# A hybrid pooling and RWKV-7 encoder: two recurrences side by side, their products by turns, with six value groups spread beside them

## The chip, the cores and the metric

The kernel runs on one core of one Trainium2 chip. TensorE (PE) multiplies, VectorE (DVE) and ScalarE (ACT) do the element-wise work and empty PSUM, GpSimd (POOL) does a few small copies, and SyncE (SP) issues most transfers. Each engine executes its own queue in order; semaphores tie the queues together. The metric is the device time of one execution in microseconds (us), as a median of runs.

## The reference

One sequence of 256 tokens of width 2048 goes through two layers. The first mixes tokens by causal pooling, the second by an RWKV-7 recurrence; each is followed by a gated feed-forward block. The part that matters here is the recurrence of the second layer:

```python
def step(state, inp):
    r_t, w_t, k_t, v_t, a_t, b_t = inp
    sa = jnp.einsum('bhvk,bhk->bhv', state, a_t)
    state = (state * w_t[:, :, None, :] + sa[..., None] * b_t[:, :, None, :]
             + v_t[..., None] * k_t[:, :, None, :])
    return state, jnp.einsum('bhvk,bhk->bhv', state, r_t)
...
_, y = lax.scan(step, state0, seq_in)
...
y = (y + bonus.reshape(B, S, D)).astype(h.dtype)
return (y * g) @ w_o
```

There are 32 heads of 64 channels. Ahead of it stand the products r, k, v of the shifted tokens with 2048 x 2048 weights, two small low-rank products for decay and a (`w_la`, `a_la`) and one for the gate (`g_la`); behind it a norm per head, the gate, and the output product with `w_o`.

## The kernel before

The recurrence is done in chunks of 64 tokens. Four heads make a group; there are eight groups, and each has a chain of four chunks in order of time. All activations of a stage stay on the chip, weights are streamed in pieces of 512 KB (`raw`), and each piece is split into a high part (ACT, line 152) and a low remainder (DVE, line 153), so that a product of two float32 numbers becomes three fast ones.

The second layer runs in this order: `keys` and `receptances` (products for k and r, 16 of each), `values` (eight groups of four pieces), `prepare` (decayed k and r of a group, written to memory as dKB and dM), `invert` (solves all 64-by-64 triangular systems of half the heads by 31 pairs of DVE instructions), `ready` (loads a group's operands back, makes its Gram matrices G and its inverses Z), `chains` (the recurrence), `head_norm` with `gating`, and `out_proj`.

One chunk of a chain has three phases, each ended by a `yield`. Phase 0 (lines 905 to 912): products of G with the values, of AR with the state S, and a copy on ACT to `rhs`. Phase 1 (lines 915 to 917): products with Z and a copy back to the value rows. Phase 2 (lines 920 to 937): products with G and with KBT, four updates of S on DVE, a scaled copy `Se`, and the copy of the result to `y`. A product in float32 is issued as two matmul instructions. Chunk c reads one half of the 128 rows where c is even and the other where it is odd (`kh[c % 2]`).

What runs beside what is written by hand. `weave(main, *others)` walks a main generator step by step; each of the others has a count of units, a first step and a last step, and is advanced evenly between them. This fixes the program order. When the program is built, each engine's queue is put in order from it: a scheduler goes by program order as priority (`high_priority(HP)` moves instructions 30 places ahead) and by its own estimate of when operands and buffers are ready. Tiles with a tag share a number of buffers and wait for a free one.

Before, a chain starts every `STAG` = 8 steps and takes 12, so that two chains are live in half of the 68 steps, out of phase. `values(0)` to `values(3)`, the low-rank gate product and `invert(0)` precede; six of the 16 units of `values(4)` to `values(7)` run just ahead of the chains and the rest by step 20 (`VL`). `out_proj` for the first two groups starts at step 26. PSUM has three banks for large accumulations (`acc`), three for `g` and two for the chains (`cb`). The tag `mx` has `MX` = 40 buffers of 128 x 512, shared by mixed inputs, r, k, KB, AR, y and others.

```python
more = [(ready(g), 6, STAG * g - STAG, STAG * g - RE) for g in range(1, 8)]
more += [(head_norm(g), 4, STAG * g + 12, STAG * g + 12 + HNL) for g in range(7)]
more += [(vals, 16 - LV, 0, VL), (prep, 28 - LP, 0, PE_), (invert(1), 18, PE_, IE), (reload(), 1, STAG + 12, STAG + 13)]
```

Of the kernel before, what the change touches and what calls it, by code (L numbers as in the profile page):

```python
# [14 lines left out]
ALU = mybir.AluOpType  # L15
# [14 lines left out]
MX = 40  # L30
# [9 lines left out]
OB_ = ((0, 2), (2, 2), (4, 2), (6, 1))  # L40
LASTO = 6
OA, OB = 0, 0
STAG, OG, RE = 8, 2, 0
BANKS = {"acc": 3, "g": 3, "cb": 2}
# [48 lines left out]
def hybrid_encoder(ctx: ExitStack, tc: tile.TileContext, I, out):  # L93
# [6 lines left out]
    base = cp.tile([128, 5120], F32, name="base")  # L100
# [149 lines left out]
    def ffn(layer, each=None):  # L250
        gcol = par[f"g2_{layer}"]
        with ExitStack() as st:
# [4 lines left out]
            rb = base[:, 4864:]  # L257
# [188 lines left out]
    def chained(*gens):  # L446
        for gen in gens:
            yield from gen

    def rwkv():  # L450
        with ExitStack() as st:
# [52 lines left out]
            def values(gi):  # L504
# [3 lines left out]
                for u in range(4):  # L508
# [135 lines left out]
            with tc.tile_pool(name="rp1", bufs=1) as p1:  # L644
# [51 lines left out]
                def loras(srcs, names, m, fns, dsts):  # L696

                    acc = acc_bank()
                    xs = None
# [85 lines left out]
                for k in range(16):  # L785
# [3 lines left out]
                      (loras(I["la"], ("mu_w", "mu_a"), 96, (AF.Tanh, AF.Copy), hid[:2]), 17, LA0, 24),  # L789
# [10 lines left out]
            Z = [c2.tile([128, 8, 64], F32, name=f"Z{q}") for q in range(3)]  # L800
# [19 lines left out]
            def ready(gi):  # L820
# [3 lines left out]
                z = Z[gi % 3]  # L824
                w11 = pt = c2.tile([128, 8, 32], F32, name="w11", tag="w11", bufs=1)
                m12 = c2.tile([128, 8, 32], F32, name="m12", tag="m12", bufs=1)
# [60 lines left out]
            def chains(gi):  # L887

                vt, z, S = vts[gi], Z[gi % 3], Sb[gi % 2]
                ar_, kbt_, g_ = AR[gi], KBT[gi], G[gi]  # L890
                y = ys_raw[gi] = mx(F32, "y")

                sv = (vt, c2.tile([128, 512], F32, name="sv", tag="sv", bufs=3))
                nc.gpsimd.tensor_copy(sv[1][kh[1]], vt[kh[1]])
                odd[gi] = sv[1]
                heads_ = [(jj, slice(hd * 64, hd * 64 + 64), jj * 2 + hd) for jj in range(2) for hd in range(2)]
                Se = None
# [268 lines left out]
```

## Time and profile before

| what | value |
|---|---|
| median of 3 runs | 2182.81 us (2179.54 to 2190.74) |
| the profiled execution | 2181.9 us, span 2180.1 us |
| mean granted TensorE clock | 0.981 |
| busy: PE, PEld, DVE, ACT, POOL | 2116.9, 1843.5, 1553.9, 1147.3, 30.6 us |

PE is the busy time of matmuls, PEld that of loads of their stationary operand, which run beside them. Matmuls overlap, so the duration of one is longer than the distance between two starts. In a row of a group of instructions stand line, engine, operation, operands, shapes and count, then busy us, mean ns, and the idle time of the engine just before with what ended it. In a row of time stand start, duration, engine, line, operation and count. A clock of 1.00 is full speed, 0.50 is half. In a row of waits stand who waited for whom, us in total, times and the longest.

### The profile page before, as it was taken

To read this page: it belongs to the slowest core of one execution; us is meant where nothing else is said; L and a number is where in the kernel's file an instruction comes from. 1 tells how busy PE (TensorE), PEld (TensorE's weight loads), DVE (VectorE), ACT (ScalarE), POOL (GpSimd) and SP (SyncE) were. 2 spreads that over 40 slices of the span, in tenths; PEclk is the share of its full clock that TensorE was granted. 3 is DMA by queue.
4 is the path that set the end of the run, shared out by engine and by line. 5 is a ranking of instruction groups with operands and counts; after the bars stand their busy time and mean duration, and the time that the engine had idled before them with its cause. 6 is when DMAs were issued, how large, how long until landed. Compare 5 with 4: busy or idle time off the path is not lost.

```text
span 2180.1 us, 34748 instructions
## 1 busy us (share of the span) xinstructions
PE 2116.9 (97%) x13318; PEld 1843.5 (85%) x13318; DVE 1553.9 (71%) x2548; ACT 1147.3 (53%) x1884; POOL 30.6 (1%) x72
## 2 busy tenths in 40 slices
PE   7999999999999989999999999999999999999997
PEld 5888888888878879999988778788888888888786
DVE  8666666666787978688866767876666666677886
ACT  5544444444555478766745354554444444445444
POOL 0000000000000000011000000000000000000000
PEclk9999999999999999999998699999999999999999
DMA  6555565665566645466565343446666666655654
GB/s 232 174 187 191 186 191 187 190 187 190 196 198 217 207 155 163 163 210 207 171 218 151 108 121 105 160 121 191 188 189 189 188 189 189 188 191 199 204 202 156
DMA packets 147478, 395.11 MB, mean 181 GB/s; under 512 B 39280, under 2 KB 46832, under 8 KB 147056
## 3 DMA queue, kind: packets, MB, share of 16 engines
q1 hardware_dynamic: 146160, 390.80, 56.2%
q8 instruction: 104, 1.70, 0.3%
q10 hardware_dynamic: 1152, 2.10, 0.3%
q14 instruction: 62, 0.51, 0.1%
HBM read 376.59 MB, written 16.25 MB: 180 GB/s over the span
## 4 chain that ended last, share of the span: by engine, by line
PE 86%; DVE 6%; DMA 4%; ACT 2%; issue 1%; SPq 0%; ACTq 0%; DVEq 0%
PE acc L311 29%; PE acc L347 17%; PE acc L313 15%; PE acc L691 2%; PE acc L689 2%; PE acc L690 2%; DVE wl L153 2%; PE tp L347 2%; PE acc L1022 1%; PE acc L1024 1%; PE acc L1023 1%; DMA raw<-in_w 1%; PE acc L516 1%; PE acc L515 1%; PE cb L907 1%
## 5 line engine op out<-in xcount | busy, mean ns | idle before, releaser
L153 DVE TENSOR_TENSOR wl<-raw,wh 128x1024 fp32r<-128x1024 f32 (+1 forms) x525 | 640.2, 1220 | 432.2 <-ACT wh L152 428.0
L152 ACT CAST wh<-raw 128x1024 fp32r<-128x1024 f32 (+1 forms) x525 | 548.5, 1045 | 648.7 <-PE acc L311 276.9
L311 PE MATMUL acc<-xs,wh 128*128 128x512 f32 x2816 | 710.6, 393 | 3.7 <-DVE xs L266 3.2
L311 PEld LDWEIGHTS acc<-xs,wh 128*128 128x128 f32 x2816 | 504.9, 189 | 94.9 <-DVE xs L266 5.1
L313 PEld LDWEIGHTS acc<-xs,wl 128*128 128x128 f32 x2816 | 384.1, 190 | 27.5
L313 PE MATMUL acc<-xs,wl 128*128 128x256 f32 x2816 | 392.7, 282 | 0.0
L347 PE MATMUL acc<-vh,gT 128*128 128x512 f32 x640 | 184.9, 390 | 0.8 <-ACT vh L152 0.8
L347 PEld LDWEIGHTS acc<-vh,gT 128*128 128x128 f32 x640 | 119.7, 188 | 27.3 <-ACT vh L152 2.6
L691 PE MATMUL acc<-mx,wl 128*128 128x256 f32 x464 | 133.0, 287 | 3.5 <-DVE wl L153 3.5
L689 PE MATMUL acc<-mx,wh 128*128 128x256 f32 x464 | 132.1, 285 | 0.0
L690 PE MATMUL acc<-mx,wh 128*128 128x256 f32 x464 | 131.8, 284 | 0.0
L153 DVE TENSOR_TENSOR vl<-raw,vh 128x1024 fp32r<-128x1024 f32 x80 | 95.5, 1221 | 27.1 <-ACT vh L152 19.7
L347 PE MATMUL acc<-vl,gT 128*128 128x512 f32 x320 | 112.2, 389 | 0.0
L152 ACT CAST vh<-raw 128x1024 fp32r<-128x1024 f32 x80 | 80.9, 1050 | 49.3 <-PE acc L347 22.7
L355 ACT CAST vh<-T 128x1024 fp32r<-128x1024 f32 x56 | 58.9, 1052 | 80.5 <-DVE T L397 43.6
L347 PE MATMUL acc<-wh,gT 128*128 128x512 f32 x320 | 93.8, 390 | 0.7 <-ACT wh L152 0.7
L691 PEld LDWEIGHTS acc<-mx,wl 128*128 128x128 f32 x464 | 88.5, 191 | 5.3 <-DVE wl L153 5.2
L689 PEld LDWEIGHTS acc<-mx,wh 128*128 128x128 f32 x464 | 88.5, 191 | 0.8
L690 PEld LDWEIGHTS acc<-mx,wh 128*128 128x128 f32 x464 | 88.6, 191 | 0.0
L347 PE MATMUL acc<-vh,g 128*128 128x512 f32 x280 | 77.9, 391 | 1.1 <-ACT vh L355 0.6
L516 PE MATMUL acc<-wl,mx 128*128 128x256 f32 x256 | 74.2, 290 | 1.2 <-DVE wl L153 1.1
L515 PE MATMUL acc<-wh,mx 128*128 128x256 f32 x256 | 74.2, 290 | 0.0
(329 smaller groups left out, 3118.5 us busy)
## 6 DMA issues: line engine op xcount, KB each, us to landing
raw<-in_w SPq DMA_DIRECT2D x528, 512.0 KB, 4.4
raw<-in_wk SPq DMA_DIRECT2D x32, 512.0 KB, 3.7
raw<-in_wr SPq DMA_DIRECT2D x32, 512.0 KB, 3.7
raw<-in_wv SPq DMA_DIRECT2D x32, 512.0 KB, 4.0
raw<-in_wo SPq DMA_DIRECT2D x32, 512.0 KB, 3.6
raw<-in_pw SPq DMA_DIRECT2D x8, 512.0 KB, 7.8
dKB<-KB SPq DMA_DIRECT2D x16, 256.0 KB, 3.1
dKB<-AR SPq DMA_DIRECT2D x16, 256.0 KB, 3.7
```

What stands on the lines that cost most here:

```text
L152: nc.scalar.copy(wh[:P, :step], raw[:P, :step])
L153: nc.vector.tensor_sub(wl[:P, :step], raw[:P, :step], wh[:P, :step].bitcast(F32))
L311: nc.tensor.matmul(acc, lhsT=w[:, cs], rhs=xs[q * 4 + kk], start=(q + kk == 0), stop=False, skip_group_check=True)
L313: nc.tensor.matmul(acc[:, :256], lhsT=l[:, cs], rhs=xs[q * 4 + kk][:, :256], start=False, stop=(q + kk == 6), skip_group_check=True)
L347: nc.tensor.matmul(out_, lhsT=lhsT, rhs=rhs, start=start, stop=stop, skip_group_check=True)
L355: nc.scalar.copy(wh, src)
L515: nc.tensor.matmul(av[:, i], lhsT=xh, rhs=w[:, cs], start=(k == 0 and i == 0), stop=False, skip_group_check=True)
L516: nc.tensor.matmul(av[:, i], lhsT=xh, rhs=l[:, cs], start=False, stop=False, skip_group_check=True)
L689: nc.tensor.matmul(acc[:, :256], lhsT=w[:, cs], rhs=xs[k][:, :256], start=(k == 0), stop=False)
L690: nc.tensor.matmul(acc[:, :256], lhsT=w[:, cs], rhs=xs[k][:, 256:], start=False, stop=False)
L691: nc.tensor.matmul(acc[:, :256], lhsT=l[:, cs], rhs=xs[k][:, :256], start=False, stop=(k == 15))
L907: nc.tensor.matmul(cb[:, jj, 0, hc], lhsT=g_[jj][u % 2][k_, c], rhs=rows_of(u)[k_], start=(u == 0), stop=False, skip_group_check=True)
```

## The change

Two lanes take the place of the staggered chains. Lane by lane, `BEGIN` gives the step at which each chain starts; chains 0 and 1 start three steps (one chunk) apart, and each next pair follows as the one before ends, so that two chains are live in all but the first and the last three of 51 steps. Both are always in the same phase and their matmuls are written alternately. `values(0)` and `values(1)` stay ahead; the other six groups are spread until step 39, six units of them just ahead of the chains. The gate's low-rank product moves from beside the first values into `keys`, on a `cb` bank. The output projection goes in blocks of two groups (`range(4 * q, 4 * q + 4)` pairs). Buffers change: `mx` 40 to 36, Z 3 to 4, `w11` and `m12` 1 to 2, `sv` 3 to 4, `Se` 2 to 3, and two places for the norm's gain row `lnx` instead of one.

```diff
-MX = 40
+MX = 36
...
-HP, VL, HNL = 30, 20, 6
-LV, LP, PE_, IE = 6, 14, 8, 16
+HP, HNL = 30, 6
+VF, LV, LP, PE_, IE = 2, 6, 14, 8, 17
+
+BEGIN = (0, 3, 12, 15, 24, 27, 36, 39)
+STEPS = 51
+READY = ((3, 12), (5, 15), (17, 24), (18, 27), (28, 36), (30, 39))
...
-                        vts[gi] = mx(F32, "vt") if gi < 4 else late[0].tile([128, 512], F32, name="vt", tag="vt", bufs=4)
+                        vts[gi] = mx(F32, "vt") if gi < VF else late[0].tile([128, 512], F32, name="vt", tag="vt", bufs=4)
...
                 weave(keys(),
-                      (loras(I["la"], ("mu_w", "mu_a"), 96, (AF.Tanh, AF.Copy), hid[:2]), 17, LA0, 24),
+                      (loras(I["la"], ("mu_w", "mu_a"), 96, (AF.Tanh, AF.Copy), hid[:2], acc_bank), 17, LA0, 22),
+                      (loras(I["ga"], ("mu_g", "mu_g"), 128, (AF.Sigmoid, AF.Sigmoid), hid[2:], cb_bank), 17, 8, 30),
                       (mixes("mu_r", xr), 16, 12, 32))
...
-                weave(chained(values(0), values(1), values(2), values(3)),
-                      (loras(I["ga"], ("mu_g", "mu_g"), 128, (AF.Sigmoid, AF.Sigmoid), hid[2:]), 17, 0, 12),
-                      (invert(0), 18, 0, 14))
+                weave(chained(*(values(g) for g in range(VF))),
+                      (invert(0), 18, 0, 4 * VF))
...
+            def chain_step(phase, lanes):
+                with tc.high_priority(HP):
+                    if phase == 0:
+                        for a in lanes:
+                            a.chunk()
                         for jj, hc, u in heads_:
+                            for a in lanes:
+                                nc.tensor.matmul(a.cb[:, jj, 0, hc], lhsT=a.g[jj][u % 2][a.k, a.c], rhs=a.rows_of(u)[a.k], start=(u == 0), stop=False, skip_group_check=True)
+                        for a in lanes:
+                            if a.c:
+                                for jj in range(2):
+                                    nc.tensor.matmul(a.cb[:, jj, 0], lhsT=a.ar[jj][:, a.c], rhs=a.S[a.c % 2][:, jj], start=False, stop=False, skip_group_check=True)
+                        for a in lanes:
+                            a.rhs = c2.tile([128, 2, 128], F32, name="rhs", tag="rhs", bufs=2)
+                            nc.scalar.copy(a.rhs[a.b], a.cb[a.b, :, 0])
+                    elif phase == 1:
                         for jj, hc, u in heads_:
+                            for a in lanes:
+                                nc.tensor.matmul(a.cb[a.b, jj, 1, hc], lhsT=a.z[a.b, u * 2 + a.i], rhs=a.rhs[a.b, jj, hc], start=True, stop=True, skip_group_check=True)
+                        for a in lanes:
+                            nc.scalar.copy(two(a.row[a.b]), a.cb[a.b, :, 1])
+                    else:
                         for jj, hc, u in heads_:
+                            for a in lanes:
+                                nc.tensor.matmul(a.cb[a.k, jj, 0, hc], lhsT=a.g[jj][u % 2][a.b, a.c, a.k], rhs=a.rows_of(u)[a.b], start=False, stop=True, skip_group_check=True)
+                        for a in lanes:
+                            if a.c < 3:
+                                for jj, hc, u in heads_:
+                                    nc.tensor.matmul(a.cb[hc, jj, 1, :64], lhsT=a.kbt[jj][:, a.c, hc], rhs=a.rows_of(u), start=True, stop=True, skip_group_check=True)
...
             def all_chains():
+                lanes = []
+                for step in range(STEPS):
+                    if step in BEGIN:
+                        lanes.append(Chain(BEGIN.index(step)))
+                    chain_step(step % 3, lanes)
+                    lanes = [a for a in lanes if a.c < 4]
                     yield
...
-                lnx = base[:, 4864:]
+                lnx = base[:, 4672 + gi % 2 * 256:][:, :256]
...
+            second = ready(1)
+            weave(itertools.islice(vals, LV), (itertools.islice(prep, LP), LP, 0, LV), (ready(0), 6, 1, LV), (itertools.islice(second, 3), 3, 3, LV))
+            ended = lambda g: BEGIN[g] + 12
+            more = [(second, 3, 0, 3)] + [(ready(g), 6, *READY[g - 2]) for g in range(2, 8)]
+            more += [(head_norm(g), 4, ended(g), ended(g) + HNL) for g in range(7)]
+            more += [(vals, 4 * (8 - VF) - LV, 0, BEGIN[7]), (prep, 28 - LP, 0, PE_), (invert(1), 18, PE_, IE), (reload(), 1, ended(1), ended(1) + 1)]
+            more += [(out_proj(range(4 * q, 4 * q + 4)), 8, ended(2 * q + 1) + HNL, min(ended(2 * q + 1) + HNL + 12, STEPS)) for q in range(3)]
+            more += [(last_weights(), 4, STEPS - 12, STEPS - 2), (head_norm(7, 0, 1), 4, STEPS - 5, STEPS)]
+            rest.append(out_proj(range(12, 14)))
             weave(all_chains(), *more)
```

The updates of S, `Se` and the copy to `y` are the same per lane as before, lane after lane.

More of the change, by code (lines that the diff above doesn't have):

```diff
@@ L97, in hybrid_encoder @@
     sm = ctx.enter_context(tc.tile_pool(name="sm", bufs=2))
-    base = cp.tile([128, 5120], F32, name="base")
+    base = cp.tile([128, 5184], F32, name="base")
     h = [[base[:, (i * 4 + n) * 512:(i * 4 + n + 1) * 512] for n in range(4)] for i in range(2)]
@@ L256, in ffn @@
             ps = st.enter_context(tc.tile_pool(name="fps", bufs=1, space=PSUM))
-            rb = base[:, 4864:]
+            rb = base[:, 4864:5120]
             xs = []
@@ L823, in ready @@
                 half, at = gi // 4, (gi % 4) * 8
-                z = Z[gi % 3]
-                w11 = pt = c2.tile([128, 8, 32], F32, name="w11", tag="w11", bufs=1)
-                m12 = c2.tile([128, 8, 32], F32, name="m12", tag="m12", bufs=1)
+                z = Z[gi % 4]
+                w11 = pt = c2.tile([128, 8, 32], F32, name="w11", tag="w11", bufs=2)
+                m12 = c2.tile([128, 8, 32], F32, name="m12", tag="m12", bufs=2)
                 AR[gi], KBT[gi], G[gi] = [], [], []
@@ L940, in all_chains, with __init__, chunk, rows_of @@
-            def all_chains():
-                live = []
-                for step in range(7 * STAG + 12):
-                    if step % STAG == 0 and step < 8 * STAG:
-                        live.append(chains(step // STAG))
-                    live = [g for g in live if next(g, g) is not g]
+            class Chain:
+                def __init__(self, gi):
+                    self.gi, self.c, self.vt, self.z, self.S = gi, 0, vts[gi], Z[gi % 4], Sb[gi % 2]
+                    self.ar, self.kbt, self.g, self.Se = AR[gi], KBT[gi], G[gi], None
+                    self.y = ys_raw[gi] = mx(F32, "y")
+                    self.sv = (self.vt, c2.tile([128, 512], F32, name="sv", tag="sv", bufs=4))
+                    nc.gpsimd.tensor_copy(self.sv[1][kh[1]], self.vt[kh[1]])
+                    odd[gi] = self.sv[1]
+                def chunk(self):
+                    q, self.i = self.c % 2, self.c // 2
+                    self.k, self.b = kh[q], kh[1 - q]
+                    self.row = self.sv[q][:, self.i * 256:(self.i + 1) * 256]
+                    self.cb = cb_bank().rearrange("p (j x c) -> p j x c", j=2, x=2)
+                def rows_of(self, u):
+                    return self.row[:, u * 64:(u + 1) * 64]
@@ L1059, in rwkv @@
             ys, ys_raw, gates, last_w, odd, rest = {}, {}, {}, [], {}, []
-            vals = chained(*(values(g) for g in range(4, 8)))
+            vals = chained(*(values(g) for g in range(VF, 8)))
             prep = chained(*(prepare(g, g_bank) for g in range(4, 8)))
@@ L1067, in reload @@
                 yield
-            assert IE <= 3 * STAG and PE_ <= IE
-            weave(itertools.islice(vals, LV), (itertools.islice(prep, LP), LP, 0, LV), (ready(0), 6, 1, LV))
-            more = [(ready(g), 6, STAG * g - STAG, STAG * g - RE) for g in range(1, 8)]
-            more += [(head_norm(g), 4, STAG * g + 12, STAG * g + 12 + HNL) for g in range(7)]
-            more += [(vals, 16 - LV, 0, VL), (prep, 28 - LP, 0, PE_), (invert(1), 18, PE_, IE), (reload(), 1, STAG + 12, STAG + 13)]
-            for first, count in OB_:
-                g = first + count - 1
-                at = STAG * g + 12 + HNL
-                if g < LASTO:
-                    more.append((out_proj(range(2 * first, 2 * g + 2)), 4 * count, at + OA, at + STAG * count + OB))
-                else:
-                    rest.append(out_proj(range(2 * first, 2 * g + 2)))
-            E_ = 7 * STAG + 12
-            more += [(last_weights(), 4, E_ - 12, E_ - 2), (head_norm(7, 0, 1), 4, E_ - 5, E_)]
+            second = ready(1)
[7 more added lines that the diff above has]
+            rest.append(out_proj(range(12, 14)))
             weave(all_chains(), *more)
```

77 lines of the change are left out of this document (21 added, 56 removed).

## The prediction

> **What bounds the kernel now.** I read the page first (busy shares, then the row of granted clocks), then the busy time by stretch, then the waits and the order of time inside the recurrence.
>
> ```profile
> PE 2116.9 (97%) x13318; PEld 1843.5 (85%) x13318; DVE 1553.9 (71%) x2548; ACT 1147.3 (53%) x1884; POOL 30.6 (1%) x72
> ...
> PEclk9999999999999999999998699999999999999999
> ```
>
> TensorE is the bound, nearly everywhere; only two slices of forty show a clock under 0.9, and both lie in the stage that the change rebuilds. The sources of lines 907 and 937 give that stage's ends, 1111 to 1409 us; the stretches around it (columns: length, then busy time of PE, PEld, DVE, ACT, POOL with counts, granted clock, DMA share, GB/s) are
>
> ```profile
> L907 PE MATMUL cb<-vt,base x32: 214/272/320, 1111.6 to 1180.5; 64*128 64x64 f32 x32
> ...
> L937 ACT COPY y<-cb x32: 348/367/369, 1141.4 to 1409.4; 64x256 f32<-64x256 f32 x32
> ...
> 805.00:912.00 107.00, 106.46 (x897) 106.26 (x896) 80.89 (x155) 87.15 (x189) 0.00 (x0) 1.00 0.48 157
> ...
> 1020.00:1050.00 30.00, 29.44 (x243) 29.04 (x243) 27.55 (x63) 19.06 (x38) 0.66 (x1) 1.00 0.57 181
> 1050.00:1111.00 61.00, 58.04 (x480) 55.61 (x479) 45.30 (x93) 38.50 (x69) 4.12 (x10) 0.97 0.62 193
> 1111.00:1409.00 298.00, 287.38 (x2665) 240.08 (x2664) 211.64 (x466) 145.30 (x315) 9.39 (x21) 0.90 0.44 136
> ```
>
> In the 298 us of the recurrence PE is idle for only 10.6 us, but its mean clock is 0.90. The loss is the clock, in three stretches:
>
> ```profile
> 1183.50:1217.60 34.10, 28.21 (x204) 23.31 (x202) 26.13 (x73) 10.63 (x25) 0.76 (x1) 0.50 0.26 71
> ...
> 1234.70:1251.80 17.10, 16.72 (x92) 13.73 (x91) 7.26 (x18) 5.46 (x13) 0.00 (x0) 0.50 0.39 110
> ...
> 1282.50:1289.30 6.80, 6.14 (x16) 4.53 (x16) 1.81 (x3) 0.84 (x3) 0.00 (x0) 0.50 0.87 248
> ...
> 1185.00:1190.00 5.00, 1.27 (x23) 0.92 (x22) 1.50 (x7) 0.65 (x2) 0.00 (x0) 0.50 0.57 112
> 1190.00:1195.00 5.00, 4.71 (x40) 4.42 (x40) 4.33 (x16) 2.55 (x5) 0.00 (x0) 0.50 0.00 0
> ```
>
> PE is busy 28.21 + 16.72 + 6.14 = 51.1 us at half clock. At full clock that is 25.5 us of work.
>
> Why there? The order of time shows a hole in the supply of independent products:
>
> ```profile
> 1170.86 0.28 PE L517 MATMUL acc<-wh,mx 128*128 128x256 f32 x1
> 1170.98 0.28 PE L515 MATMUL acc<-wh,mx 128*128 128x256 f32 x1
> 1171.10 0.28 PE L516 MATMUL acc<-wl,mx 128*128 128x256 f32 x1
> 1171.22 0.28 PE L517 MATMUL acc<-wh,mx 128*128 128x256 f32 x1
> ...
> 1190.29 1.11 PE L921 MATMUL cb<-sv,base 64*64 64x64 f32 x8 [4.01 <-ACT sv L917]
> ...
> 1211.48 0.79 PE L1022 MATMUL acc<-wh,ys 128*128 128x512 f32 x1
> ```
>
> The last product of the eight value groups is issued at 1171, the first of the output projection at 1211. In those 40 us PE has only the recurrence and its preparation, and the recurrence is a chain of short hops between PE, ACT and DVE. One late transfer then stops it:
>
> ```profile
> DVE sysP L633 <- DMA sysM<-dM: 7.3, 1, 7.3
> ...
> ACT ysq L980 <- DVE sysZ L634: 6.2, 1, 6.2
> ...
> PE cb L921 <- ACT sv L917: 4.0, 1, 4.0
> PE g L840 <- DMA KB<-dKB: 2.9, 3, 1.9
> ...
> PE cb L907 <- ACT y L937: 0.9, 1, 0.9
> ```
>
> The second inversion's first DVE instruction waits 7.3 us for its matrix at the head of DVE's queue; the square of the head norm waits behind it on ACT; the recurrence's copy (line 917) is queued behind that square; PE waits 4.0 us for the copy, from 1186.3 to 1190.3. The clock had fallen 3 us earlier, at 1183.5, among short products alone, and stays at half until the projection's long products are running.
>
> **The change, part by part.** The profiled execution took 2181.9 us (span 2180.1), 0.9 under the median of the runs, 2182.81; the sum is made on 2181.9.
>
> *Filler spread.* Before, the ten remaining value units are due by step 20 of 68 and the projection starts at step 26. After, eighteen units run to step 39 of 51 and the projection's first quarter is due from step 21, so the hole closes. Two value groups are 2 x 96 products; the rows above show them 0.12 us apart, so 23 us of PE work moves into the recurrence, out of the stretch before it: no PE time is added or saved. What is gained is the clock, at most 25.5 us. The inversion's wait of 7.3 us stays, though: it still follows the last preparation at step 8, and behind it on DVE stand the subtractions that the value units themselves need, so filler cannot cover all of it. I leave 7.5 us of loss for one cold stretch there and take **-18** (ends 0 and -25.5).
>
> *Idle time.* 10.6 us of PE idle in the stage; the 4.0 us and part of the 2.9 us go with better filling. The double-buffered gain row (line 972), four Z tiles instead of three and two w11/m12 pairs let the preparation run earlier. I take **-4** (ends +5 and -8).
>
> *Products by turns.* Lanes one chunk apart read opposite 64-row halves. The trace has both orders:
>
> ```profile
> 1364.18 1.10 PE L907 MATMUL cb<-vt,G 64*128 64x64 f32 x8
> 1365.21 0.68 PE L916 MATMUL cb<-rhs,Z 64*64 64x64 f32 x8
> 1365.82 0.50 PE L1023 MATMUL acc<-wl,ys 128*128 128x512 f32 x1
> ...
> 1351.36 1.16 PE L853 MATMUL g<-AR,KB 64*128 64x128 f32 x16
> 1352.45 0.38 PE L916 MATMUL cb<-rhs,Z 64*64 64x64 f32 x3
> 1352.62 0.27 PE L921 MATMUL cb<-sv,G 64*64 64x64 f32 x1
> ...
> 1353.23 0.25 PE L875 MATMUL g<-w,m 32*32 32x32 f32 x4
> ```
>
> Eight of line 907 on one half take 1.03 us to the next start, and sixteen of the same weight shape (line 853) with halves alternating take 1.09. Eight of line 916 take 0.61 us; eight of it and eight of line 921, mostly by turns, take 0.78 (1352.45 to 1353.23) instead of 1.22. So one round of two lanes saves 0.97 us on line 907 and 0.44 each on lines 916 and 921: 1.85 us. Both lanes run in steps 3 to 47, 15 rounds: 28 us if every product finds its partner. It won't: the copies that release the two lanes follow one another on ACT (0.37 us each), and the builder places a product as soon as its own lane is ready, so a lane can go ahead alone. The end at zero is an order in which no pair forms. I take **-13**, about half, because PE has a backlog in most of the stage and both lanes are then ready when their turn comes (ends 0 and -28).
>
> [...]
>
> *Gate projection moved into the keys* (16 steps of two loads-and-splits plus one mix, 96 products of 0.12 us):
>
> ```profile
> L676 ACT ACTIVATE mixa<-hn,misc 128x256 f32<-128x256 f32 x84 | 42.1, 507 | 0.0
> L159 ACT CAST mx<-mix 128x256 fp32r<-128x256 f32 x96 | 37.1, 405 | 6.9 <-DVE mix L677 6.8
> ...
> L705 ACT CAST lwh<-lraw 128x256 fp32r<-128x256 f32 x16 | 6.0, 400 | 6.4 <-DMA lraw<-in_ga 6.4
> ```
>
> PE's 11.5 us moves with it, for nothing net. But ACT gets 16 x (507 + 405 + 400) ns = 21 us more in a stage where it is busy 87.15 of 107: 108 of a stage of then 118 us, 92%, beside the weight casts. The cover is nearly gone; its 16 loads on SP's queue are small beside the weights there. I take **+3** (ends 0 and +10). In the place that it leaves, DVE was the tight one (27.55 of 30 us) and PE idled 3.5 us in 91: **-2** (ends 0 and -3.5).
>
> *Four mixed-tile slots fewer* (40 to 36). In the receptances 16 xr, 4 + 4 paired outputs, up to 16 xv and the KB/AR pair of the preparation no longer fit from about step 24 on, so the last preparation of the first half, and with it the first inversion, can wait for an xr tile of the last receptance. Value products cover most of that wait. **+2** (ends 0 and +10).
>
> Sum: -18 - 4 - 13 + 3 - 2 + 2 = -32, so 2181.9 - 32 = **2150 us**. The last stretch and both feed-forward blocks are untouched.
>
> **The rivals.**
>
> *Pairs and clock both in full.* -25.5 - 8 - 28 + 3 - 2 + 2 = -58: 2123 us. For it: the by-turns rows above. Against it: the ready times of the lanes differ.
>
> *Only idle stretches count for the clock.* If the clock falls only after a long idle stretch, the closed hole takes all three cold stretches with it: -25.5 for -18, 2142 us. Against it: the first stretch begins before the 4.0 us wait; the second, at 1234.7, has no PE wait near it longer than the 0.9 us for line 937; and at 1190 to 1195 PE is busy 4.71 of 5 us and stays at half clock. So a thin mix of short products seems enough to make and keep it cold. [...]
>
> *The change hardly pays.* The inversion's wait still stops DVE, so the value units stop too; the clock falls again for as long (-5 of 25.5), pairs do not form (-4), and the crowded keys cost what the better filling saves: about 2173 us.
>
> *Slower: the round becomes the bound.* Two lanes share two cb banks, so a lane's next chunk cannot start line 907 before its last chunk's copy and state update are done; before, the second bank let it start early.
>
> ```profile
> 1172.46 0.71 PE L910 MATMUL cb<-S,AR 128*128 128x128 f32 x4
> ...
> 1174.84 0.45 PE L925 MATMUL cb<-vt,KBT 128*64 128x64 f32 x8
> ```
>
> ```profile
> L153 DVE TENSOR_TENSOR wl<-raw,wh 128x1024 fp32r<-128x1024 f32 x521 | 637.5, 1224 | 429.9 <-ACT wh L152 425.6 <-ACT t L315 3.6
> ...
> L930 DVE SCALAR_TENSOR_TENSOR S<-cb,misc,Se 64x64 f32<-64x64 f32 x64 | 18.1, 283 | 9.3 <-PE cb L925 8.4
> ...
> L912 ACT COPY rhs<-cb 64x256 f32<-64x256 f32 x32 | 11.7, 366 | 23.6 <-PE cb L910 19.6 <-PE cb L907 3.6
> ```
>
> A round of two lanes: lines 907 2.1, 916 and 921 1.2 each without pairs, 910 and 925 2 x (0.71 + 0.45) = 2.3, six ACT copies 2.2, eight DVE updates 2.3: 11.3 us, 17 rounds 192 us, against 298 + 23 - 32 = 289 us, 17.0 us a round. The room is 5.7 us; four hops each behind one 1.22 us subtraction take 4.9. It decides at (298 + 23)/17 = 18.9 us a round, where nothing is gained. With each hop behind two (21.1 us) the stage takes 359 us, 38 more: about 2220 us. A nearer case, 20 us, gives 2200. Against it: DVE is busy only 211.64 of 298 us.
>
> **How the numbers follow.** Runs of this kernel tell about 0.5% (11 us) from no change. Forecast, 2130 to 2170: 0.60. Both in full: 0.12. Clock rule, 2142: 0.07, inside the forecast's range. Hardly pays: 0.13, of which most lies within 0.5%. Slower: 0.08. Faster by over 0.5% is the first three, 0.79, less a little: 0.77; same 0.13; slower 0.10. The range leaves out the slower case and the far half of the full one: 2118 to 2178.
>
> **What the next profile would show.** Clock: the stage's granted clock at 0.95 or more, with half-clock stretches of under 20 us together. Filling: no span over 10 us without value or projection products. Turns: line 907 in runs of 16 near 1.1 us; if in runs of 8 near 1.0, that term is zero. Keys: ACT near 90% and PE still at 99%. The forecast is wrong if line 633 still waits 7 us and 30 us of half clock follow, or if PE's waits for lines 912, 917 and 930 sum to more than 20 us.

## The result, and the profile after

The changed kernel takes 2215.9 us (median of 4 runs, 2215.1 to 2216.2) against 2182.4 us for the kernel before beside it: a ratio of 1.0147 (95% interval 1.0119 to 1.0174). The prediction had 2150 us and a range to 2178.

Busy time and granted clock, from the page of the changed kernel:

```profile
PE 2142.3 (97%) x13318; PEld 1865.8 (84%) x13318; DVE 1557.9 (70%) x2548; ACT 1145.9 (52%) x1883; POOL 31.7 (1%) x73
...
PEclk9999999999999999999985899999999999999999
```

The matmuls are the same 13318. Their busy time grew by 25.4 us (2116.9 before), the idle time in the span of 2214.0 us by 8.5; together they are the whole difference of 33.9 us between the two profiled executions. The stretches (columns as before: length, busy time of PE, PEld, DVE, ACT, POOL with counts, granted clock, DMA share, GB/s), with four of the stretches of half clock:

```profile
805.00:930.00 125.00, 120.64 (x990) 119.78 (x989) 100.28 (x204) 105.95 (x239) 0.00 (x0) 0.97 0.45 147
1038.00:1110.00 72.00, 66.62 (x564) 64.02 (x563) 53.50 (x106) 32.09 (x44) 7.46 (x18) 1.00 0.61 182
1110.00:1442.00 332.00, 317.77 (x2726) 267.52 (x2727) 218.24 (x479) 151.95 (x331) 9.77 (x21) 0.86 0.43 131
1110.00:1123.60 13.60, 12.60 (x62) 12.20 (x63) 7.32 (x18) 6.68 (x17) 1.13 (x4) 0.50 0.67 187
1147.50:1154.30 6.80, 6.50 (x66) 6.21 (x67) 6.05 (x14) 5.87 (x16) 1.50 (x1) 0.50 0.16 37
1161.20:1178.20 17.00, 16.12 (x104) 14.10 (x105) 5.90 (x16) 5.00 (x16) 0.53 (x2) 0.50 0.43 134
1185.10:1222.60 37.50, 36.60 (x290) 33.12 (x291) 24.42 (x66) 12.60 (x31) 1.71 (x3) 0.50 0.40 106
```

The clock of the recurrence is 0.86 instead of 0.90. From 1040 to 1470 us the clock record has 99 us of half clock (61 before), and PE is busy in nearly all of it: 36.60 of the longest 37.50 us. It is not waiting for a wait to end; it runs, at half speed. The order of time there shows on what:

```profile
1161.95 1.11 PE L929 MATMUL cb<-rhs,Z 64*64 64x64 f32 x8 [1.09 <-ACT Z L883]
1162.99 1.96 PE L918 MATMUL cb<-vt,base 64*128 64x64 f32 x8
1164.88 1.22 PE L922 MATMUL cb<-S,AR 128*128 128x128 f32 x4
1166.03 1.11 PE L935 MATMUL cb<-vt,base 64*64 64x64 f32 x8
1167.08 0.69 PE L939 MATMUL cb<-vt,KBT 128*64 128x64 f32 x8
1167.70 1.12 PE L839 MATMUL g<-base,KB 128*128 128x128 f32 x4
...
1178.38 0.27 PE L935 MATMUL cb<-vt,base 64*64 64x64 f32 x1
1178.43 0.22 PE L929 MATMUL cb<-rhs,Z 64*64 64x64 f32 x1
1178.49 0.22 PE L935 MATMUL cb<-vt,base 64*64 64x64 f32 x1
1178.49 0.22 PE L929 MATMUL cb<-rhs,Z 64*64 64x64 f32 x1
```

Short products, one kind behind another. Eight of line 918 (line 907 before) take 1.89 us to the next start, where eight of line 907 took 1.03 us at full clock. No value product stands here: the values ran ahead and then stopped. The copies that end the eight groups, before and after:

```profile
L520 ACT COPY vt<-acc x8: 587/587/589, 1035.7 to 1171.6; 128x512 f32<-128x512 f32 x8
```

```profile
L520 ACT COPY vt<-acc x8: 585/585/588, 1051.6 to 1363.4; 128x512 f32<-128x512 f32 x8
```

The last group now ends at 1363 us, but six of the eight are done by 1143. By the trace, 576 of the 768 value products start ahead of the first set of products with the inverse Z (line 929, at 1143 us), 24 more by 1155 us, and the next one only at 1239 us; before, 619 start ahead of the first set (line 916, at 1132 us) and the other 149 by 1171 us. The counts that the expectations give as ahead of "the first product with the inverse" (600, and 672 before) are by the trace those ahead of the second set. The first product of the output projection starts at 1232 us. So the hole without value or projection products is 77 us (1155 to 1232) where it was 40.

### The profile page after: what moved, and what is told of

Read it like the earlier page. It is cut to its first block, busy times and chain, and to the rows that moved or that the text cites. A ratio compares the mean times of both kernels' runs of the same rounds, so it can differ in the third digit from the quotient of the medians.

```text
span 2214.0 us, 34788 instructions
## 1 busy us (share of the span) xinstructions
PE 2142.3 (97%) x13318; PEld 1865.8 (84%) x13318; DVE 1557.9 (70%) x2548; ACT 1145.9 (52%) x1883; POOL 31.7 (1%) x73
## 4 chain that ended last, share of the span: by engine, by line
PE 83%; DVE 7%; DMA 4%; ACT 3%; issue 2%; SPq 0%; ACTq 0%; DVEq 0%
PE acc L311 29%; PE acc L347 15%; PE acc L313 15%; PE acc L691 2%; PE acc L689 2%; PE acc L690 2%; DVE wl L153 2%; PE tp L347 1%; DMA raw<-in_wv 1%; DMA raw<-in_w 1%; ACT wh L152 1%; PE cb L918 1%; PE acc L1038 1%; PE acc L1039 1%; PE acc L1040 1%
```

## The experiments

Four theories were put to the test. H1: the values ran ahead and left the longer hole, and that cost the time. H2: the early part cost it (gate product among the keys, four slots fewer, later inversion). H3: two `cb` banks for two lanes make the round the bound. C: TensorE's clock follows how many columns it moves in a window of 3.41 us.

All stretches of half clock in these traces, except the one in which each trace ends, are whole multiples of 3.41 us (in the clock records before and after, from 3.413 to 37.547 us), so I cut each trace into such windows and counted in each the moving columns of its matmul records (a few per cent of the records may be missing). In the table, half clock and idle are those from 1040 to 1470 us of the profiled execution (idle: of the whole span); the last column is PE's busy time less half of what it was busy at half clock, over the whole span. The half is an estimate: in the changed kernel value products start 0.21 us apart at half clock (1119.75 to 1123.16 us) and 0.12 at full (1125.98 to 1127.89), 1.8 times as far. A profile is one execution: that of the lanes with 40 slots is the fastest of ten, that with short products added the slowest of four.

| kernel | median us | ratio (95%) | profiled span | half clock | PE idle | PE busy, as at full clock |
|---|---|---|---|---|---|---|
| before | 2182.4 | | 2180.1 | 61 | 63 | 2087 |
| after | 2215.9 | 1.0147 (1.0119–1.0174) | 2214.0 | 99 | 72 | 2089 |
| lanes, early part undone, 36 slots | 2200.8 | 1.0073 (1.0050–1.0097) | 2199.0 | 89 | 59 | 2094 |
| the same, 40 slots | 2181.0 | 0.9983 (0.9957–1.0009) | 2170.2 | 38 | 58 | 2093 |
| after, gate product back | 2212.6 | 1.0138 (1.0118–1.0157) | 2210.5 | 123 | 66 | 2083 |
| after, lane by lane | 2234.3 | 1.0213 (1.0169–1.0257) | 2229.0 | 133 | 73 | 2089 |
| before, 36 slots | 2199.7 | 1.0074 (1.0047–1.0100) | 2202.2 | 85 | 60 | 2099 |
| before, gate product in keys | 2200.6 | 1.0072 (1.0050–1.0095) | 2205.6 | 85 | 65 | 2095 |
| after, values held | 2242.3 | 1.0243 (1.0202–1.0284) | 2251.1 | 157 | 79 | 2093 |
| before, values held | 2195.7 | 1.0047 (1.0024–1.0070) | 2188.8 | 58 | 61 | 2098 |
| before, long products added | 2187.4 | 1.0015 (0.9996–1.0034) | 2190.4 | 38 | 54 | 2116 |
| before, short products added | 2215.8 | 1.0141 (1.0088–1.0193) | 2225.8 | 113 | 58 | 2110 |
| after, long products added | 2209.1 | 1.0122 (1.0106–1.0137) | 2211.9 | 75 | 73 | 2102 |

The last column carries the finding: without added products it is 2083 to 2099 us in every kernel of the study, with the same 13318 matmuls, while the half clock goes from 38 to 157 us. What the edits changed is in the main how much of the work ran at half clock, and some idle time. The column is not quite constant: with 36 slots in the kernel before it is 12 us higher, nearly as much as the clock costs there (28 us more of busy time at half clock, so 14 us). Where that comes from is not shown.

**Undoing parts.** Lanes with the early part of before (`VF` = 4, gate product beside the first values, late values due by step 15), first with 36 slots, then with 40:

```diff
-VF, LV, LP, PE_, IE = 2, 6, 14, 8, 17
+VF, LV, LP, PE_, IE = 4, 6, 14, 8, 17
...
-(vals, 4 * (8 - VF) - LV, 0, BEGIN[7])
+(vals, 4 * (8 - VF) - LV, 0, 15)
```

> The changed kernel with its early part put back: four groups of values precede the loop, the gate product stands beside the first values instead of among the keys, and the late values are due by step 15; the lanes, the rounds and the 36 slots stay. H1: the values are all queued before the second round as before the change, so that the hole is about as long as it was, 40 us, and the time is 2182 to 2197 us. H2: the whole loss goes, 2175 to 2187 us, and the last receptance is back within 4 us of 1019.8 us. H3: it stays, 2205 to 2220 us.

> The last lanes kernel (early part put back, values due by step 15) with 40 slots of the shared ring instead of 36, so that of the change only the lanes and their rounds remain. It stands at 2200.8 us with 36 slots, and the kernel before went from 2182 to 2199.7 us by the slots alone. Theory S (the four slots are what the rest of the loss is): 2180 to 2190 us. Theory L (the lanes cost the 18 us by themselves, and the slots cost nothing in this kernel): 2196 to 2205 us. In both, by the theory that the clock follows how many columns TensorE moves, the time goes with the half clock of the stage from 1040 to 1470 us: 61 us of it at S, 88 us at L.

2200.8 and 2181.0 us. The lanes with their rounds and 40 slots cost nothing that can be told from the kernel before, and H3 falls: in the changed kernel PE waits 4.4 us in all for the copy of `y` behind which a lane's next chunk stands, and the `y` copies span 16 rounds in 285.9 us, 17.9 each.

```profile
PE cb L918 <- ACT y L953: 4.4, 4, 2.7
...
PE cb L935 <- ACT vt L931: 1.4, 1, 1.4
```

```profile
L953 ACT COPY y<-cb x32: 355/367/368, 1156.0 to 1441.9; 64x256 f32<-64x256 f32 x32
```

The slots alone and the gate product alone, in the kernel before, and the gate product put back in the changed kernel:

```diff
-MX = 40
+MX = 36
```

> The kernel before with 36 slots of the shared ring instead of 40, nothing else. H2 with the slots as its main part: slower by 6 to 15 us (2188 to 2197 us). H1 and H3: within 4 us of the kernel before (2178 to 2187 us); the prediction's term was +2 us with a bound of +10.

```diff
+(loras(I["ga"], ("mu_g", "mu_g"), 128, (AF.Sigmoid, AF.Sigmoid), hid[2:], cb_bank), 17, 8, 30),
...
-(loras(I["ga"], ("mu_g", "mu_g"), 128, (AF.Sigmoid, AF.Sigmoid), hid[2:]), 17, 0, 12),
```

> The kernel before with the gate product moved among the keys as in the change, on a cb bank, with 40 slots and four groups of values ahead of the loop as before. Theory G (the gate product among the keys is what the early part costs): 2190 to 2198 us, with TensorE waiting for ACT and DVE at the mixes and a half clock near 891 us. The rival (it only moves, and the products saved beside the first values give it back): 2179 to 2187 us; then the late values are what is left of the changed kernel's early part.

> The changed kernel with the gate product back beside the first values, as before the change; two groups precede, six late ones, 36 slots and the lanes stay. The kernel before lost 17.5 us by the gate product among the keys alone, 17.6 us by the four slots alone, and the lanes with 40 slots stand at 2181.0 us. Theory A (these two are the whole loss and the late values cost nothing): 2196 to 2203 us. Theory V (the six late groups of values cost the 15 us that lie between the lanes with 36 slots, 2200.8 us, and the changed kernel): 2211 to 2219 us.

The slots cost 17.7 us by themselves and the gate product 17.5, each with 24 us more half clock in the recurrence, where the prediction had put no cost for them. They do not add: from the lanes with 40 slots (2181.0) the slots cost 19.8 us, the late values (with the first inversion, which moves with them) then 11.8 (to 2212.6), and the gate product the last 3.3, which the intervals do not tell from nothing. So H2 is half right (the early part costs), and its mechanism is not the one it named. With 36 slots the builder puts 719 value products ahead of the second set of products with the inverse and 49 behind it, instead of 672 and 96. With the last group held back so that it is 672 and 96 again (due by step 8), 2193.7 us and 72 us of half clock: between the two ends, so the order may be a part of it. The interval (1.0016 to 1.0070) overlaps with that of the slots alone, so that this is not shown.

```diff
+with queued("chain") if "chain" in last and gi == 7 else nullcontext():   # around a value unit's products
```

> The kernel before with 36 slots, and the last group of values queued behind the newest recurrence product, due by step 8: by its queue 672 value products stand ahead of the first product with the inverse and 96 in the round after it, as with 40 slots (719 and 49 with 36 slots alone, 2199.7 us). Theory Q (the slots cost through this order alone): 55 to 70 us of half clock in the stage and 2178 to 2188 us. The rival (fewer slots cost elsewhere): 2194 to 2204 us.

The products of the two lanes one lane after the other, in all three phases:

```diff
-for jj, hc, u in heads_:
-    for a in lanes:
+for a in lanes:
+    for jj, hc, u in heads_:
```

> The changed kernel with the products of the two lanes issued lane after lane in each step instead of by turns, nothing else. The prediction's term (turns are worth 13 us): 2223 to 2232 us. The theory that turns hardly form, since the lanes are not ready together (7 of 256 first products started within 30 ns of the one of the other lane): 2212 to 2220 us.

2234.3 us: turns are worth 18 us (four runs from 2225.7 to 2239.3 us against 2215.1 to 2216.2). But the work as at full clock is 2089 us with and without, and one product is as long (from 1300 to 1360 us, at full clock nearly throughout, after and lane by lane):

```profile
L929 PE MATMUL cb<-rhs,Z 64*64 64x64 f32 x56 | 4.8, 227 | 0.0
```

```profile
L929 PE MATMUL cb<-rhs,Z 64*64 64x64 f32 x48 | 3.7, 224 | 0.0
```

What they give is clock: 34 us less of half clock in the stage. PE was busy at half clock for 26 us less over the span, which is 13 of the 15 us between the two profiles.

**Long against short products in the hole.** Added to the kernel before, results unread: 56 products of 128x512, then 98 of 64x64 (196 matmuls, 12,544 columns; the expectation counted each product once).

```diff
+for _ in range(WN):
+    nc.tensor.matmul(acc, lhsT=hid[2][:, :128], rhs=hid[3], start=True, stop=True, skip_group_check=True)
```

> The kernel before with 56 added products of 128x512 whose results nobody reads, in the two rounds between the last value product and the first product of the output projection (1171.6 to 1211.5 us). By the row of the output projection's products (419 to 444 ns) they are about 24 us of TensorE work. The clock theory (a stretch of short products alone is what brings the half clock, whatever the idle share): the half clock between 1183 and 1270 us goes, the granted clock of that stretch is over 0.9, and the 20 to 25 us that it cost pay for the added work: 2176 to 2190 us. The rival (the half clock comes from the total of work in the stage or from idle time, not from the kind of products): the half clock stays and the added work is paid in full, 2198 to 2210 us.

```diff
-nc.tensor.matmul(acc, lhsT=hid[2][:, :128], rhs=hid[3], ...
+nc.tensor.matmul(acc[:64, :64], lhsT=hid[2][:64, :64].bitcast(F32), rhs=hid[3][:64, :64].bitcast(F32), ...
```

> The kernel before with 98 added products of 64x64 in plain float32 whose results nobody reads, where the 56 added products of 128x512 stood; by the rows of the recurrence's 64x64 products (233 to 241 ns) they are about the same 24 us of TensorE work, but they move 6,272 columns where the others moved 28,672. Theory C (the half clock follows the columns moved): the hole stays under 3,000 columns a window, 50 us of half clock or more in the stage stay, the added work is paid and partly doubled, and the time is 2196 to 2220 us. The rival (any work that keeps TensorE from idling holds the clock): under 40 us of half clock and 2178 to 2192 us, as with the long ones (2187.4 us).

The stretch of the hole, 1180 to 1240 us, in the kernel before, with long and with short products added:

```profile
1180.00:1240.00 60.00, 51.74 (x452) 42.91 (x449) 42.19 (x117) 23.00 (x51) 1.42 (x3) 0.67 0.39 113
```

```profile
1180.00:1240.00 60.00, 59.15 (x593) 48.96 (x587) 43.48 (x119) 25.89 (x63) 1.87 (x3) 0.94 0.45 130
```

```profile
1180.00:1240.00 60.00, 60.00 (x462) 51.70 (x457) 27.08 (x75) 16.40 (x41) 2.33 (x4) 0.53 0.31 78
```

With the short ones PE is busy 60.00 of 60 us and the clock is 0.53, lower than with 8 us of idle time; with the long ones it is 0.94. The added rows are

```profile
L1065 PE MATMUL acc<-hid 128*128 128x512 f32 x56 | 15.9, 408 | 0.0
```

```profile
L1065 PE MATMUL acc<-hid 64*64 64x64 f32 x196 | 23.3, 288 | 0.0
```

(23.3 us, mostly at half clock; at full clock, by eight of line 916 in 0.61 us, they would be 15). So 15.9 us of added long work cost 5 us against the kernel before run beside it, which its interval does not tell from nothing, and short work of about the same size 31. Being busy did not hold the clock: 60.00 busy us of 60 ran at 0.53. The 31 us are not the price of the short products alone, though. In that queue the first product of the output projection also stands further back, behind eleven sets of products with the inverse instead of eight, and starts at 1262 us (1212 with the long ones, 1211 before), so the hole is longer too. And the short products differ from the long ones in more than their columns: their stationary operand is 64*64, where that of the long ones is 128*128 (the rows above), and they are plain float32, where the long ones are not.

In the kernel before, the stretches of half clock that the prediction lists are 6.8, 17.1 and 34.1 us: 2, 5 and 10 times 3.413 us. With the short products added the clock fell and stayed down with PE busy throughout: 60.00 of 60 us above, and 70.00 of the 70 us ahead of it, at 0.97.

**Spreading the values.** In the changed kernel, each late unit queued behind the newest product of the recurrence, so that it cannot run ahead, the last due by step 30. Then, in the changed kernel again, long products added and queued in that way; its values are not held.

```diff
+with queued("chain") if "chain" in last else nullcontext():   # around a value unit's products
...
-nc.tensor.matmul(a.cb[a.b, jj, 1, hc], ...
+last["chain"] = nc.tensor.matmul(a.cb[a.b, jj, 1, hc], ...
```

> The changed kernel with one edit: the products of each late group of values are queued on TensorE behind the newest recurrence product at their place in the program, so that they can't be issued ahead of it, and the last of them is due at step 30. In the changed kernel itself 600 of the value products stand before the first product with the inverse and then none for four rounds; here it is 399, and 24 to 72 in each round after that. Theory H1 (the values ran ahead, and the hole between 1155 and 1235 us without a long product is what cost the time): the half clock between 1110 and 1250 us goes, some 44 us shrink to under 15 us, and the time falls by 15 to 30 us, to 2186 to 2201 us. H2 (the early part, that is the gate product among the keys, four slots fewer and the later inversion, cost the time): 2208 to 2216 us. H3 (two banks for two lanes make the round the bound): the rounds get longer by the products that now stand in them, 2214 to 2230 us.

```diff
+with queued("chain"):
+    for _ in range(WN):   # 12 times 5, steps 1 to 13
+        nc.tensor.matmul(acc, lhsT=hid[2][:, :128], rhs=hid[3], start=True, stop=True, skip_group_check=True)
```

> The changed kernel with 60 added products of 128x512 whose results nobody reads, queued behind the newest recurrence product from step 1 to step 13; they push the value products back too (386 ahead of the first product with the inverse, then 42, 36, 16, 48, 58), so that it stands nearest to the kernel with the values held, which has 399 and 57, 24, 48, 41, 37 and takes 2242.3 us with 157 us of half clock. The added work is about 25 us (419 to 444 ns each). Theory C: the half clock of the stage falls under 90 us, and the time is 2215 to 2240 us although there is more to do. The rival (the rounds of two lanes are the bound, or thin rounds stay cold whatever is added): 2255 to 2280 us.

From 1110 to 1180 and from 1180 to 1240 us, first the changed kernel with its values held, then with long products added instead:

```profile
1110.00:1180.00 70.00, 67.09 (x519) 57.09 (x520) 31.67 (x73) 27.25 (x69) 4.01 (x15) 0.62 0.34 106
1180.00:1240.00 60.00, 59.29 (x447) 51.36 (x446) 27.77 (x64) 20.10 (x43) 2.12 (x4) 0.59 0.38 110
```

```profile
1110.00:1180.00 70.00, 65.58 (x547) 55.42 (x548) 32.81 (x77) 31.57 (x82) 3.20 (x15) 0.70 0.35 110
1180.00:1240.00 60.00, 60.00 (x607) 51.20 (x606) 39.00 (x102) 23.64 (x53) 1.79 (x3) 0.94 0.46 137
```

H1 holds in part as a cause (the late values cost 11.8 us) and falls as a remedy: with 24 to 64 value products from one set of products with Z to the next, up to 1296 us, PE is busy 126 of 130 us and runs at about 0.6, 2242.3 us. So many value products, 3 to 8 us by their 0.12 us in rounds of 16 to 36 us, were too thin a mix here. The changed kernel with 60 products more to do is 7 us faster than without them (2207.5 to 2213.7 us against 2215.1 to 2216.2). In the profiled executions its work as at full clock is 13 us more and its idle time 1.5, but it is busy at half clock for 33 us less, which saves 16. The added products also push value products back (384 ahead of the first set with Z, 576 in the changed kernel); in the kernel with the values held, which has 360 there, the half clock was longer and not shorter. That the loss of the changed kernel goes through the clock is thereby seen in that kernel itself.

**Placing the values better.** If a window needs some 3,000 columns (an estimate from counts such as those in the last section), the right dose of value products in the hole should gain. Four kernels start from the kernel before, three from the lanes with 40 slots. "Held" is the edit above: `with queued("chain")` around the products of a unit.

All ten late units held, still due by step 20:

```diff
+with queued("chain") if "chain" in last else nullcontext():
```

> The kernel before with one edit: the late value products are queued on TensorE behind the newest recurrence product at their place in the program, still due by step 20. By its queue 576 of them (672 before) stand before the first product with the inverse, and 72, 24, 51, 45 in the next rounds (96, 0, 0, 0 before). Theory C (in the traces so far, of 509 windows of 3.41 us at full clock in which TensorE moved 3,500 columns or more none was followed by a window of half clock, and of 28 with under 2,500 columns 25 were): the hole between 1180 and 1240 us, now at 2,427 columns a window, comes to over 3,300, the stretch ahead of it falls from 4,990 to about 4,000 and stays above the edge, the half clock of the stage shrinks from 61 us to under 25 us, and the time is 2160 to 2173 us. The rival (spreading the values costs by itself, as in the changed kernel with them spread, 2242 us, since they no longer cover the wait for the inversion): TensorE idles 8 us or more in 1040 to 1130 us, and the time is 2182 to 2200 us.

The last two groups in pieces of six products, each piece held, steps 1 to 16:

```diff
+pieces = chained(*(values(g, True) for g in range(6, 8)))
...
+(vals, 4 * (6 - 4) - LV, 0, 2), (pieces, 16 * (8 - 6), 1, 16),
```

> The kernel before with the products of its last two groups of values cut into pieces of six, each queued behind the newest recurrence product of its place, due from step 1 to step 16. By its queue 618 value products stand ahead of the first product with the inverse and 66, 36 and 48 in the rounds after it (672, 96, 0 and 0 before). Theory C (a window of 3.41 us needs some 3,000 moved columns to keep the full clock): the hole of 1180 to 1240 us rises from 2,427 columns a window to about 3,600, the stretch ahead of it falls from 4,990 to about 3,900, both above the edge; the half clock of the stage falls from 61 us to under 30 us and the time to 2163 to 2176 us. The rival (there are too few long products for the whole stretch, so that what the hole gains the rounds ahead of it lose, as when the pieces were whole units: 2195.7 us): 58 us of half clock or more, 2182 to 2198 us.

The last group held, then the last six units, both with the values due by step 12:

```diff
+with queued("chain") if "chain" in last and gi == 7 else nullcontext():
```

> The kernel before, 40 slots, with the last group of values queued behind the newest recurrence product and due by step 12: 672 value products ahead of the first product with the inverse, then 39 and 57 (96 and 0 before). The lanes with 40 slots have 673, 45 and 50, and had 37.5 us of half clock. Theory C: 30 to 48 us of half clock and 2168 to 2179 us. The rival (what one round gains the other loses): 55 us or more and 2180 to 2192 us.

```diff
+with queued("chain") if "chain" in last and gi * 4 + u >= 26 else nullcontext():
```

> The same with the last six units of values held, due by step 12: 624 ahead of the first product with the inverse, then 96 and 48. Theory C: the round after the inversion keeps its 96 and the next gets 48 from the dense stretch ahead, 25 to 45 us of half clock and 2165 to 2177 us, if TensorE doesn't idle for what the 48 covered; the rival (they covered the wait for the inversion): over 6 us more idle time between 1040 and 1130 us and 2182 to 2194 us.

In the lanes: the last two units held; the last group in held pieces; and 12 times two long products added:

```diff
+with queued("chain") if "chain" in last and gi * 4 + u >= 30 else nullcontext():
```

> The lanes with 40 slots and the early part of before (2181.0 us), with the last two units of values (48 products) queued behind the newest recurrence product: its queue has 45, 2, 18 and 30 value products in the rounds after the first product with the inverse, against 45, 50, 0 and 0. Theory C: round two loses what rounds three and four gain; the half clock stays within 15 us of the 37.5 us it had, 2174 to 2188 us. The rival (a later last value is better in itself): half clock under 20 us and 2160 to 2172 us.

```diff
+pieces = chained(*(values(g, True) for g in range(7, 8)))
...
+(vals, 4 * (7 - VF) - LV, 0, 2), (pieces, 16 * (8 - 7), 1, 15),
```

> The lanes with 40 slots and the early part of before, the last group of values in pieces of six behind the newest recurrence product, due from step 1 to step 15: its queue has 696 value products ahead of the first product with the inverse (673 there) and 12, 24, 24 and 12 after it (45, 50, 0, 0). Theory C: 12 products of 256 columns are some 560 columns for each of a round's five and a half windows; with only two thirds as many long products behind the first round, spread thin, the half clock grows over 50 us and the time is 2184 to 2198 us. The rival (even spreading holds the clock): half clock under 25 us, 2160 to 2174 us.

```diff
+WU, WN = 12, 2
...
+(warmth(), WU, 8, 15),   # as in the kernel before
```

> The lanes with 40 slots and the early part of before (2181.0 us, 37.5 us of half clock), with 24 added products of 128x512 whose results nobody reads, due from step 8 to step 15: some 10 us of TensorE work. By its queue 31, 38 and 28 value products and 4, 4, 6, 8 and 2 added ones stand in the rounds ahead of the first product of the output projection. Theory C: the windows there rise by some 700 columns to over 3,500, the half clock falls under 20 us and the idle time by 3 to 6 us: 2168 to 2180 us, ahead of both kernels. The rival (the added work costs what the clock gains, as it did in the kernel before): 2182 to 2194 us.

They gave 2195.7, 2185.4, 2199.2, 2190.9, 2212.1, 2208.3 and 2197.7 us (ratios 1.0047, 1.0011, 1.0060, 1.0028, 1.0117, 1.0114 and 1.0067); in the same order 58, 55, 102, 58, 143, 72 and 65 us of half clock. None is ahead of the kernel before, and most of my numbers were misses, as were several before them: the values held, the lanes with 36 slots and the slots with the order put back (0.3 us short of its rival's range) came out in none of the ranges named for them, the slots alone, the gate product alone and lane by lane 2 to 3 us above the nearest, and the long products in the changed kernel 6 us below. Where they missed here, it was mostly the half clock again that differed; with the last group in pieces in the lanes, half of the 29 us between the two profiles is idle time (72 us against 58). In the kernel with ten units held the hole rose from 2,427 to 4,036 columns a window, and the 70 us ahead of it fell from 4,990 to 3,601 on average, with 8 of 20 windows under 3,000. A mean above the estimated edge was not enough there, since units come in lumps. And the counts of value products per round do not decide it: the last group held leaves 672, 39 and 57, the lanes with 40 slots 673, 45 and 50, and they had 102 and 38 us of half clock (the second slowest and the fastest of ten executions; the medians are 18 us apart). What also moves with each edit (recurrence, `ready`, projection) is not in that count. A rule by which one could place the products by hand was not found.

## Why the prediction was wrong, step by step

*Filler spread, −18: the step that failed, twice.* First, the spread did not come about: the queue that the builder makes put the values ahead, and the hole grew from 40 to 77 us. Second, the premise was wrong. The prediction read "a thin mix of short products seems enough to make and keep it cold" from 1190 to 1195 us, and then took it that a thin admixture of long ones would cure it. Held in place, they made 157 us of half clock. Instead of -18 the clock came out at +24: half of the 47.5 us more that PE was busy at half clock over the whole span, of which 21 in the recurrence and 3 elsewhere, in the main in the keys. Not all of that is the spread: it alone, undone, was 11.8 us, with 34 us of half clock, and the slots and the gate product add to the rest.

*Idle time, −4:* in the recurrence, of which the term spoke, +3.6 (14.2 of 332 us idle against 10.6 of 298): inside the bounds, the other way. Over the whole span it is +8.5; part of that is the keys stage (PE busy 120.64 of 125 us at 0.97).

*Products by turns, −13:* undone, they cost 18.3 us, so the size is near, but the mechanism was not seen. Eight and eight in 0.78 us needs both lanes ready. Products on opposite halves did start within 0.01 us of each other where both were ready (line 918 at 1123.94 and 1124.10 us, from `vt` and `sv`). But after 1124 us no product of line 918 stands by turns with one on the other half; 24 of its groups are plain runs of eight. No product is shorter, and the gain is clock. The stated sign, runs of eight, was to mean a term of zero: that was wrong too.

*Gate product into the keys, +3 (0 to +10), and slots, +2 (0 to +10):* 17.5 and 17.7 us alone. Both were costed in the keys, the receptances and the preparation. Most of their price arises later, in the recurrence, where the half clock is 24 us longer; that the shifted order of the values does it is likely and not shown, and the slots are also those of KB, AR and y, which the recurrence uses. In the changed kernel the gate product costs at most a few us: such prices are not sums.

*Room left by the gate product, −2:* not tried alone.

*Slower, by the round:* right side, wrong mechanism. The waits for the copies are a few us, and the rounds are 17.9 us long with PE busy 317.77 of 332.

*"Only idle stretches count for the clock":* refused by the 60.00 busy us at 0.53.

*Signs.* Stage clock 0.86 for 0.95 expected; 99 us of half clock for under 20; a hole of 77 us; ACT in the keys 105.95 of 125, 85%. Line 633 waits only 3.0 us now (7.3 before), less than the prediction feared, and the half clock came all the same:

```profile
DVE sysP L633 <- DMA sysM<-dM: 3.0, 1, 3.0
```

Left open: why turns lessen the half clock, by which moves the slots and the gate product lengthen it, and why the work as at full clock differs by up to 16 us between kernels.

## What to carry to other kernels

Where TensorE bounds a stage, take its busy time apart by granted clock first: here edits that left its work alone moved the time by up to 2.4%, in the main through the clock. Here long products held the clock where they stood dense (0.94 from 1180 to 1240 us with 56 of 128x512 added) and not where they stood thin beside short ones (about 0.6 with 24 to 64 value products a round), and moved columns told more of it than busy time (0.53 with PE busy 60.00 of 60 us): keep such products dense and count columns (which of them count in full is open, as said below). A term priced where an edit sits is not its price if a builder puts the queues in order; compare the order of the queue before and after.

## What the runs showed of the hardware

In these traces the clock went with what was moved in the window before. Over all twenty traces, from 1040 to 1470 us: of 1,715 windows at full clock with 3,500 or more moved columns 3 were followed by one at half; of 52 with under 2,000 all were; between, 35 of 46 (2,000 to 2,500), 33 of 77 (to 3,000) and 23 of 126 (to 3,500). Busy time did not sort them so: in some 1,700 of the windows at full clock PE was busy for over 98% of the time, and 67 of these were followed by one at half. At half clock, 274 of 276 windows under 2,500 stayed there and 3 of 91 from 3,500 on. By the rows of the prediction a window full of line 916 (eight in 0.61 us) would move 2,865 columns and one full of line 907 (eight in 1.03 us) 1,697: line 907 alone would lose the full clock even without a gap, and line 916 alone stands in the band where 33 of 77 windows were followed by half clock, while value products at 0.12 us move 7,280. This is an estimate from those rows and counts. Columns weighted by the size of the stationary operand (64*64 as a quarter of 128*128) sort the windows nearly as well: in the traces before and after, where 13 of 203 windows at full clock were followed by one at half, the best edge leaves 5 on the wrong side (1,300 weighted columns), against 3 for plain columns (2,700). So which of the two is counted stays open; whether the type of the products counts was not tested.

Executions of one kernel differ by it as well: the lanes with 40 slots ran from 2172.2 us at a mean clock of 0.988 to 2194.9 us at 0.976.
